# A hybrid attention layer on one core: the sample's dots in a pinned order, branch 3's loads, and three narrower products per sum of values

## The chip, the core and the metric

The kernel runs on one core of a Trainium2 chip. The metric is the device time of one launch in microseconds, the median of several runs. A core has five engines that work in their own order each: PE (TensorE, the matmuls), DVE (VectorE), ACT (ScalarE), POOL (GpSimd) and SP (SyncE, which here issues all transfers between the device's memory and the core's). An engine takes its instructions strictly in the order in which they stand; if the first of them waits, all behind it wait too.

## The reference, cut to what matters

One step of a one-layer decoder. 2048 prompt rows and 64 sample rows (8 sequences of 8) are normed and multiplied by one matrix; its columns feed an attention mixer of 8 heads (q, k, v), a gated linear attention (qb, kb, vb, g) and two gates; both mixers go through an output projection.

```python
DILATED = ((128, 1), (512, 4), (2048, 16))

def dilated_branch_sample(q, k_buf, v_buf, window, dil):
    ...
    idx = W + jnp.arange(T)[:, None] - dil * jnp.arange(n_keys)[None, :]
    ...
    kg = k_buf[:, idx]
    vg = v_buf[:, idx]
    s = jnp.einsum('bthd,btnhd->bthn', q, kg) * (hd ** -0.5)
    s = jnp.where(valid[None, :, None, :], s, -jnp.inf)
    return softmax_attend(s, vg, 'bthn,btnhd->bthd')

def dilated_mixture(results):
    outs = jnp.stack([r[0] for r in results], axis=0)
    lses = jnp.stack([r[1] for r in results], axis=0)
    alpha = jax.nn.softmax(lses, axis=0)
    return jnp.einsum('gblh,gblhd->blhd', alpha, outs)
```

The prompt is attended in the same three branches (window and dilation), each query with the keys of its own residue. For the sample, each of 64 rows is multiplied with the cached keys of its branch: those dots, for branches 2 and 3, are what the kernel calls `sample_scores`.

## The kernel before

The prompt is worked in 16 tiles of 128 rows and in four groups `m` of four tiles. `project` multiplies a tile with one column block: 8 steps of K, three matmuls each, since every number is held as a high and a low half in f16 (high x high, high x low, low x high). `first(m)` runs the blocks v, q and k of a group; `rest` runs qkb, then g and vb in turn, then gb. Between the steps of `project`, `pump` advances the attention by one step, at a rate set by `credit` and by the shares given to `weave`.

Attention is a list of items. An item is `attend`: `qk` (L402) multiplies queries and keys on PE, takes mask and minimum on DVE (L416) and the exponential on ACT (L419); `tr` (L423) turns the probabilities on PE (L426) and splits them into two f16 halves, in turn by ACT and DVE (L388, L389) or by ACT and POOL (L391 to L393); `pv` (L436) multiplies them with the values (L441). A unit of branch 1 or 2 has two items of two heads, a residue of branch 3 two items of four heads; the pipeline holds three items at a time and runs an item's `pre` (its loads) one item ahead. The values lie in memory as 64 high and 64 low columns a head, so L441 multiplies 128 columns with the high and with the low half of the probabilities and leaves 128 columns, which `added` (L452) folds: ACT copies the low half (L457), DVE adds it to the high one (L458).

Branch 3 (`branch3`, L931) loads in `pre` a transposed tile of queries, one of keys and one of values, and swaps the halves of the queries on DVE (`swapped`, L845 and L846). Its pool has two buffers a tile.

The sample's dots are 64 turns (sequence b, row t). A turn loads the row's queries `qb` to all partitions (L990), the branch 3 keys `k3` (L992) and, every second turn, the branch 2 keys `k2` (L995); POOL multiplies into one buffer `pr` (L980), and DVE sums it over the 64 columns of a head (L981), first for branch 3, then for branch 2. `dot_next` takes one or two turns after each projection of groups 2 and 3, the rest run with `qkb`.

The order on each engine is not the order of the text: a scheduler places every instruction when its own timing has its inputs and buffers ready.

Of the kernel before, what the change touches and what calls it, by code (L numbers as in the profile page):

```python
# [18 lines left out]
P = 128  # L19
# [33 lines left out]
def tile_hymba(ctx: ExitStack, tc: tile.TileContext, A: dict):  # L53
# [52 lines left out]
    ident8 = cp.tile([P, P], F32, name="ident8")  # L106
    DVE.tensor_scalar(ident8[:], ident[:], 0.125, None, ALU.mult)

    ident64 = cp.tile([P, 64], F32, name="ident64")
    for r0 in (0, 64):  # L110
        DVE.tensor_copy(ident64[r0 : r0 + 64], ident8[r0 : r0 + 64, r0 : r0 + 64])
# [202 lines left out]
    def by16(ap, r):  # L314
        return ap.rearrange("(i r) c -> r i c", r=16)[r]
# [3 lines left out]
    def chain(*gens):  # L319
        for g in gens:  # L320
            yield from g
# [27 lines left out]
    with ExitStack() as c1:  # L349
# [45 lines left out]
        def attend(tag, nh, nb, scores, mask, vf, nmf, denf, OT, pre=None, post=None, neg=-1.0):  # L395
# [40 lines left out]
            def pv():  # L436
                for i in range(nh):
                    o_ = OT(i)
                    for n in range(2 * nb):
                        b, c = divmod(n, 2)  # L440
                        PE.matmul(  # L441
                            o_, t["pt"][:, c, (i * nb + b) * P : (i * nb + b + 1) * P], vf(i, b),
                            start=(n == 0), stop=(n == 2 * nb - 1),
                        )
# [7 lines left out]
        def added(out, O):  # L452

            o4 = O.rearrange("p (h c d) -> p h c d", c=2, d=HD)
            split_[0] += 2
            l = ptp.tile([P, 4, HD], F32, name=f"ol_{split_[0]}", tag="ol", bufs=1)
            ACT.activation(l[:], o4[:, :, 1], AF.Copy)  # L457
            DVE.tensor_tensor(out, o4[:, :, 0], l[:], ALU.add)  # L458


        xs, early = {}, []
# [381 lines left out]
        def swapped(q):  # L843

            DVE.tensor_copy(q[0:64, 1], q[64:128, 0])  # L845
            DVE.tensor_copy(q[64:128, 1], q[0:64, 0])  # L846
# [11 lines left out]
        def unit(m, pp, br, x):  # L858
# [30 lines left out]

            def OT(i):  # L890
                if "O" not in T:
                    T["O"] = ps_O.tile([P, 512], F32, name=f"O_{br}_{m}_{pp}_{x}", tag="O")
                return T["O"][:, i * P : i * P + P]
# [34 lines left out]
            return out  # L928


        def branch3(r):  # L931
            T = {}

            def pre():
                q = T["q"] = b3.tile([P, 2, NH, P], F16, name=f"T3_q_{r}", tag="Tq")
                SP.dma_start_transpose(q[:, 0], by16(qp_d, r))
                k = T["k"] = b3.tile([P, NH, P], F16, name=f"T3_k_{r}", tag="Tk")
                SP.dma_start_transpose(k[:], by16(kp_d, r))
                swapped(q)
                yield  # L940
                T["v"] = b3.tile([P, 1024], F16, name=f"v3_{r}", tag="v3")
                SP.dma_start(T["v"][:], by16(vp_d[:], r))
                T["o"] = b3.tile([P, NH, 66], F32, name=f"o3_{r}", tag="o3")

            def OT(a, i):
                if ("O", a) not in T:
                    T["O", a] = ps_O.tile([P, 512], F32, name=f"O3_{r}_{a}", tag="O")
                return T["O", a][:, i * P : i * P + P]

            def post(a):  # L950
                added(
                    T["o"][:].rearrange("p (i a) d -> p i a d", a=2)[:, :, a, 0:64], T["O", a][:]
                )
                if a:
                    SP.dma_start(by16(o3_d[:], r), T["o"][:].rearrange("p h d -> p (h d)"))

            return [
                attend(
                    f"3_{r}_{a}", 4, 1,
                    lambda i, a=a: [  # L960
                        (T["q"][:, order_, 2 * i + a], T["k"][:, 2 * i + a])
                        for order_ in range(2)
                    ],
                    m3,
                    lambda i, b, a=a: T["v"][:, (2 * i + a) * P : (2 * i + a + 1) * P],
                    lambda i, a=a: T["o"][:, 2 * i + a, 65:66],
                    lambda i, a=a: T["o"][:, 2 * i + a, 64:65],
                    lambda i, a=a: OT(a, i),
                    pre=None if a else pre, post=lambda a=a: post(a), neg=scl["s"][:],
                )  # L970
                for a in range(2)
            ]
# [2 lines left out]
        q_s = q_d[S : S + NS, :]  # L975
        sk_state = {}

        def dot(out, kt, qt, tag):
            pr = sk.tile([P, 512], F32, name=f"pr_{tag}", tag="pr", bufs=1)
            POOL.tensor_tensor(pr[:], kt, qt, ALU.mult)  # L980
            DVE.tensor_reduce(  # L981
                out, pr[:].rearrange("p (u k d) -> p u k d", u=2, k=4), AX.X, ALU.add
            )

        def sample_scores(b, t):
            if t == 0:
                sk_state["sc"] = sk.tile([P, 2, 64], F32, name=f"sck_{b}", tag="sc")
            sc = sk_state["sc"]
            qt = sk.tile([P, 512], F32, name=f"qb_{b}_{t}", tag="qbc")
            SP.dma_start(qt[:], q_s[8 * b + t : 8 * b + t + 1, :].to_broadcast([P, 512]))  # L990
            k3 = sk.tile([P, 512], F32, name=f"k3_{b}_{t}", tag="k3")
            SP.dma_start(k3[:], ck[b].rearrange("(m r) c -> r m c", r=16)[t])  # L992
            if t < 4:
                k2 = sk.tile([P, 512], F32, name=f"k2_{b}_{t}", tag="k2", bufs=1)
                SP.dma_start(k2[:], ck[b, W - 512 : W, :].rearrange("(j r) c -> r j c", r=4)[t])  # L995
                sk_state["k2"] = k2
            out = sc[:].rearrange("p g (u t k) -> p g t u k", u=2, t=8)[:, :, t]
            dot(out[:, 1], k3[:], qt[:], f"3_{b}_{t}")
            dot(out[:, 0], sk_state["k2"][:], qt[:], f"2_{b}_{t}")
            if t == 7:  # L1000
                SP.dma_start(sc_d[b * P : (b + 1) * P, :], sc[:].rearrange("p g c -> p (g c)"))

        nwa = kp.tile([P, KT], F32, name="nwa")
        ACT.activation(nwa[:], nw[:], AF.Abs)
# [10 lines left out]
        def q_place(k):  # L1015

            pool, tag = ((sp, "s"), (ptp, "pt"), (sk, "k3"))[k // 3]
            return pool.tile([P, 512], F32, name=f"wr_q_{k}", tag=tag)[:]

        fetch_w("q", places=q_place)  # L1020
        with tc.manual_schedule(engines={mybir.EngineType.Activation}):
# [40 lines left out]

        from collections import deque

        work, side = deque(), deque()

        def pipeline():

# [25 lines left out]
        def pump():  # L1094
            return next(pipe) is not False
# [34 lines left out]
            return (2 if name == "g" else 1) * (NT * KT + 2)  # L1130


        credit = rate = 0.0

        def dot_next(t):
            for _ in range(1 + (t != "s" and t % 2)):
                if side:
                    side.popleft()()

        def first(m):  # L1140
            tiles = list(range(4 * m, 4 * m + 4))
# [17 lines left out]
            for t in tiles:  # L1159
                for name in "vqk":  # L1160
                    if (name, t) == ("q", 15):
                        at_once(load_w("qkb"))
                    yield from project(name, [t])
                    dot_next(t)
                if t < 12:
                    prep(t + 4)
                if t < 8:
                    fetch(t + 8)
# [4 lines left out]
        for m in range(4):  # L1173
            for _ in first(m):
                credit += 3 * rate
                while credit >= 1:
                    credit -= 1
                    pump()
            for pp in range(2):
                for br in (1, 2):  # L1180
                    for x in range(4):
                        work.extend(unit(m, pp, br, x))
            rate = 0.62
            if m == 1:
                for b in range(8):
                    for t in (0, 4, 1, 5, 2, 6, 3, 7):
                        side.append(lambda b=b, t=t: sample_scores(b, t))
        c_first.close()


# [19 lines left out]
        def dots():  # L1210
            while side:
                side.popleft()()
                yield

        att = [attention(), 5.2 * len(work)]
        host = [rest("qkb"), steps("qkb")]
        weave(host, att, [chain(load_w("g"), load_w("vb")), 4 * KT], [dots(), len(side) + 3])
        c_b3.close()
        c_dot.close()
        c_att.close()  # L1220
# [667 lines left out]
```

## Time and profile before

| | us |
|---|---|
| median of 3 runs | 1423.52 (1422.46 to 1428.86) |
| the profiled execution, as a run | 1426.68 |
| its span in the trace | 1424.9 |
| mean granted clock of TensorE | 0.966 |
| idle time of POOL just before L980 | 184.9 |
| idle time of DVE just before L981 | 44.0 |

The page lists busy time by engine, the chain that ended last, and groups of instructions. In a group's row the name left of `<-` is what it writes, then its shape; behind the bar stand its busy time, the mean of one in ns, and the engine's idle time just before it with what ended most of it. Buffer numbers are left out, so `k` stands for `k2` and `k3`.

### The profile page before, as it was taken

What the parts mean: (1) busy time and instruction counts of PE and PEld (TensorE: products, weight loads), DVE (VectorE), ACT (ScalarE), POOL (GpSimd) and SP (SyncE); (2) the same over time, 40 slices, a digit from 0 to 9 for tenths busy, and PEclk for the clock granted to TensorE, in tenths of its full rate; (3) what the DMA queues carried; (4) which work ended last, traced back from release to release, by engine and by line L of the source; (5) the groups of instructions that cost most, each with busy time, mean ns of one, the idle gap of its engine ahead of it and who ended that gap; (6) DMA issues with size and microseconds to landing.
All of it is one profiled execution on the core that took longest, in us unless ns stands there. A gap on an engine that the chain in (4) does not pass through costs nothing.

```text
span 1424.9 us, 26506 instructions
## 1 busy us (share of the span) xinstructions
PE 1285.0 (90%) x8942; PEld 743.6 (52%) x8942; DVE 1018.0 (71%) x2459; ACT 843.7 (59%) x2259; POOL 621.9 (44%) x564
## 2 busy tenths in 40 slices
PE   5989999889898898996889999889999989999997
PEld 2434555455455554664667666666555434444343
DVE  6797697789798967666775357898877797773222
ACT  6466787667377775875677665777876542221120
POOL 0144355566577455554421486556551264340000
PEclk9999999999999899997999999999999999999998
DMA  8469756678966797888976444242235759998661
GB/s 297 156 188 255 192 161 150 182 203 215 240 165 173 208 288 239 260 217 228 234 190 179 149 123 116 87 153 91 88 119 176 267 179 344 359 316 267 221 215 63
DMA packets 246874, 283.27 MB, mean 199 GB/s; under 512 B 117889, under 2 KB 148690, under 8 KB 246738
## 3 DMA queue, kind: packets, MB, share of 16 engines
q1 hardware_dynamic: 246738, 281.57, 67.1%
q8 instruction: 71, 1.16, 0.4%
q14 instruction: 65, 0.53, 0.1%
HBM read 183.19 MB, written 75.24 MB: 181 GB/s over the span
## 4 chain that ended last, share of the span: by engine, by line
PE 35%; DVE 25%; DMA 16%; ACT 11%; issue 7%; POOL 4%; SPq 2%; DVEq 0%; POOLq 0%; ACTq 0%
PE Y L1488 7%; PE acc_g L1120 3%; PE acc_vb L1120 3%; PE acc_k L1120 3%; DMA k<-in_cache_k_win 2%; POOL pr L980 2%; PE s L408 2%; PE OS L1737 2%; PE acc_qkb L1120 2%; ACT p L419 2%; DMA o_d<-o 2%; DMA oc<-o_d 2%; DVE p L416 2%; PE acc_v L1120 2%; DMA T_q<-qp_d 2%
## 5 line engine op out<-in xcount | busy, mean ns | idle before, releaser
L980 POOL TENSOR_TENSOR pr<-k,qb 128x512 f32<-128x512 f32 x128 | 171.8, 1342 | 184.9 <-DVE sck L981 113.9
L1120 PEld LDWEIGHTS <-hr 128*128 128x128 f16 x1824 | 177.7, 100 | 138.2 <-issue 17.6
L419 ACT ACTIVATE p<-p,o 128x256 f32<-128x256 f32 (+1 forms) x384 | 173.1, 453 | 86.0 <-DVE o L416 83.3
L1120 PEld LDWEIGHTS <-hl 128*128 128x128 f16 x1248 | 123.2, 100 | 146.6 <-issue 22.2
L1488 PE MATMUL Y<-w_o,mh 128*128 128x512 f16 x768 | 182.9, 385 | 8.3 <-ACT mh L1454 4.9
L416 DVE CUSTOM_DVE_ANT_0 p<-s,m3w,scl_s 128x256 f32<-128x256 f32 (+1 forms) x384 | 143.6, 419 | 39.0 <-DMA o_d<-o 20.3
L393 POOL TENSOR_TENSOR pt<-p,pt 128x512 f16<-128x512 f32 (+1 forms) x80 | 98.3, 1229 | 139.6 <-ACT pt L392 107.3
L441 PE MATMUL O<-v,pt 128*128 128x128 f16 x1200 | 116.1, 224 | 25.3 <-POOL pt L393 10.0
L426 PE MATMUL t<-ident,p 128*128 128x128 f32 x600 | 119.0, 289 | 14.5 <-ACT p L419 9.2
L1488 PEld LDWEIGHTS <-mh 128*128 128x128 f16 x768 | 72.5, 99 | 103.7 <-issue 25.2
L408 PE MATMUL s<-kk,qq 128*128 128x256 f16 (+1 forms) x512 | 105.7, 326 | 17.5 <-DVE o L416 12.4
L981 DVE TENSOR_REDUCE sck<-pr 128x8 f32<-128x512 f32 x128 | 87.0, 680 | 44.0 <-POOL pr L980 43.7
L441 PEld LDWEIGHTS <-pt 128*128 128x128 f16 x1200 | 86.6, 101 | 54.6 <-POOL pt L393 13.6
L1120 PE MATMUL acc_g<-w_g,hr 128*128 128x272 f16 (+1 forms) x768 | 103.3, 285 | 1.9 <-DVE so_g L677 1.0
L1120 PE MATMUL acc_v<-w_v,hl 128*128 128x512 f16 x384 | 99.5, 405 | 4.6 <-DMA hl<-ht 3.7
L426 PEld LDWEIGHTS t<-ident,p 128*128 128x128 f32 x600 | 73.5, 146 | 43.2 <-ACT p L419 26.4
L1120 PE MATMUL acc_q<-w_q,hl 128*128 128x512 f16 x384 | 92.0, 380 | 1.9 <-ACT zs_q L703 1.4
L1120 PE MATMUL acc_k<-w_k,hl 128*128 128x512 f16 x384 | 91.3, 382 | 2.5 <-ACT w_k L658 1.3
L1454 ACT ACTIVATE mh<-tm 128x1024 f16<-128x1024 f16 x32 | 31.7, 1019 | 104.1 <-PE tm L1453 97.7
L1120 PE MATMUL acc_gb<-w_gb,hr 128*128 128x512 f16 x384 | 90.0, 388 | 2.1 <-DVE so_gb L677 2.1
L1120 PE MATMUL acc_vb<-w_vb,hr 128*128 128x512 f16 x384 | 89.3, 379 | 1.6 <-DVE so_g L677 1.6
L212 ACT ACTIVATE E<-D_e 128x256 f32<-128x256 f32 (+1 forms) x168 | 67.7, 411 | 27.1 <-DVE ks L219 17.6
(533 smaller groups left out, 2628.1 us busy)
## 6 DMA issues: line engine op xcount, KB each, us to landing
k<-in_cache_k_win SPq DMA_DIRECT2D x104, 256.0 KB, 4.3
sv<-in_cache_v_win SPq DMA_DIRECT2D x104, 256.0 KB, 5.4
hr<-h_d SPq DMA_DIRECT2D x44, 512.0 KB, 4.1
qb<-q_d SPq DMA_DIRECT2D x64, 256.0 KB, 4.6
oc<-o_d SPq DMA_DIRECT2D x48, 264.0 KB, 5.8
o_d<-o SPq DMA_DIRECT2D x64, 132.0 KB, 3.9
x<-in_x_prompt SPq DMA_DIRECT2D x16, 512.0 KB, 5.8
h_d<-hl SPq DMA_DIRECT2D x16, 512.0 KB, 4.7
```

The lines of the kernel that those rows point to most:

```text
L212: ACT.activation(E[rows, i, :n], D[rows, half], AF.Exp, scale=1.0 / 16.0)
L393: POOL.tensor_tensor(l, f, h, ALU.subtract)
L408: PE.matmul(s_ps[:, i * w : (i + 1) * w], q, k, start=(n == 0), stop=(n == len(prods) - 1),)
L416: DVE.tensor_tensor_reduce(s[:, sl], s_ps[:, sl], mask, neg, BIG, ALU.add, ALU.min, nmf(i))
L419: ACT.activation(s[:, sl], s[:, sl], AF.Exp, bias=nmf(i), scale=-1.0, accum_out=denf(i))
L426: PE.transpose(p_ps[:, i * P : (i + 1) * P], t["s"][:, i * P : (i + 1) * P], ident[:])
L441: PE.matmul(o_, t["pt"][:, c, (i * nb + b) * P : (i * nb + b + 1) * P], vf(i, b), start=(n == 0), stop=(n == 2 * nb - 1),)
L980: POOL.tensor_tensor(pr[:], kt, qt, ALU.mult)
L981: DVE.tensor_reduce(out, pr[:].rearrange("p (u k d) -> p u k d", u=2, k=4), AX.X, ALU.add)
L1120: PE.matmul(z, a_[:, k, :], w[:, p_, k, cols], start=(k == 0 and i == 0), stop=(k == KT - 1 and i == 2),)
L1454: ACT.activation(mhl[:, a], pt[:], AF.Copy)
L1488: PE.matmul(Y[:], a_[:, k, :], w_[:, part, k, :512], start=(i == 0), stop=(i == len(prods) - 1),)
```

## The change

Four things are edited, and a constant is built without a helper tile. First, the values: per block of keys three products of 64 columns (high x high, high x low, low x high) go to one 64-column sum, so `added` is gone and ACT copies the sum into `o`. The product of the two low halves is no longer formed.

```diff
             def pv():
...
-                    for n in range(2 * nb):
-                        b, c = divmod(n, 2)
+                    prods = [(b, *cd) for b in range(nb) for cd in ((0, 0), (0, 1), (1, 0))]
+                    for n, (b, c, d) in enumerate(prods):
                         PE.matmul(
-                            o_, t["pt"][:, c, (i * nb + b) * P : (i * nb + b + 1) * P], vf(i, b),
-                            start=(n == 0), stop=(n == 2 * nb - 1),
+                            o_, t["pt"][:, c, (i * nb + b) * P : (i * nb + b + 1) * P],
+                            vf(i, b)[:, d * HD : (d + 1) * HD],
+                            start=(n == 0), stop=(n == len(prods) - 1),
                         )
...
-            ACT.activation(l[:], o4[:, :, 1], AF.Copy)
-            DVE.tensor_tensor(out, o4[:, :, 0], l[:], ALU.add)
...
-                added(T["o"][:, :, 0:64], T["O"][:])
+                ACT.activation(T["o"][:, :, 0:64], T["O"][:], AF.Copy)
```

Second, branch 3 asks for a residue's tiles one residue (two items) earlier, and its values come as two tiles from the pool of branch 2's.

```diff
+        def load3(r):
+
+            T = T3[r] = {}
+            for nm_, src, shape in (("q", qp_d, [P, 2, NH, P]), ("k", kp_d, [P, 1, NH, P])):
+                t = T[nm_] = b3.tile(shape, F16, name=f"T3_{nm_}_{r}", tag=f"T{nm_}")
+                SP.dma_start_transpose(t[:, 0], by16(src, r))
+            T["v"] = []
+            for i in range(2):
+                v = vp.tile([P, 512], F16, name=f"v3_{r}_{i}", tag="v2", bufs=11)
+                SP.dma_start(v[:], by16(vp_d[:, 512 * i : 512 * i + 512], r))
...
             def pre():
-                q = T["q"] = b3.tile([P, 2, NH, P], F16, name=f"T3_q_{r}", tag="Tq")
-                SP.dma_start_transpose(q[:, 0], by16(qp_d, r))
...
+                if r == 0:
+                    load3(0)
+                    yield
+                T.update(T3[r])
+                swapped(T["q"])
+                if r < 15:
+                    load3(r + 1)
                 yield
```

Third, the dots are one generator: a turn sums the turn before, asks for the next turn's loads, and multiplies in place. Loads and sums are pinned: each stands on its engine behind all that the text has put on that engine so far.

```diff
+            def load(b, t):
+                qt = sk.tile([P, 512], F32, name=f"qb_{b}_{t}", tag="qbc", bufs=3)
+                k3 = sk.tile([P, 512], F32, name=f"k3_{b}_{t}", tag="k3", bufs=3)
...
+                for to, of in asked:
+                    tc.keep_in_program_order(SP.dma_start(to[:], of))
...
+                    tc.keep_in_program_order(
+                        DVE.tensor_reduce(
...
+            for i, (b, t) in enumerate(turns):
...
+                if last:
+                    sums(*last)
+                if i + 1 < len(turns):
+                    now = load(*turns[i + 1])
+                POOL.tensor_tensor(k3[:], k3[:], qt[:], ALU.mult)
+                POOL.tensor_tensor(qt[:], k2[:], qt[:], ALU.mult)
+                last = b, t, sc, (qt, k3)
+                yield
```

Turns are taken step by step, 1.5 to 8 steps of a projection, instead of one or two behind it. Fourth, in `rest` each further block runs a tile behind the first.

```diff
+                for g in side:
+                    dots += 1.5 / KT
+                    if dots >= 1:
+                        dots -= 1
+                        next(g, None)
...
-            for t in ["s"] + order[names[0]]:
-                for name in names:
-                    yield from project(name, [t])
+            tiles = ["s"] + order[names[0]]
+            for i in range(len(tiles) + len(names) - 1):
+                for j, name in enumerate(names):
+                    if 0 <= i - j < len(tiles):
+                        yield from project(name, [tiles[i - j]])
```

What this makes of the engines' order, at the places that the prediction speaks of. POOL, in the middle of the dots (sequence 4; `pt` is the low half of an item's probabilities), before:

```order
L980 TENSOR_TENSOR pr_3_4_4_5873<-k3_4_4_5871,qb_4_4_5869 128x512
L393 TENSOR_TENSOR pt_1_3_0_0_1_6478<-p_1_3_0_0_1_6389,pt_1_3_0_0_1_6478 128x512
L980 TENSOR_TENSOR pr_2_4_4_5876<-k2_4_0_5861,qb_4_4_5869 128x512
L980 TENSOR_TENSOR pr_3_4_1_6014<-k3_4_1_6010,qb_4_1_6008 128x512
L393 TENSOR_TENSOR pt_1_3_0_1_1_6566<-p_1_3_0_1_1_6486,pt_1_3_0_1_1_6566 128x512
L980 TENSOR_TENSOR pr_2_4_1_6017<-k2_4_1_6012,qb_4_1_6008 128x512
```

and now:

```order
L1033 TENSOR_TENSOR k3_4_4_5975<-k3_4_4_5975,qb_4_4_5974 128x512
L1034 TENSOR_TENSOR qb_4_4_5974<-k2_4_0_5816,qb_4_4_5974 128x512
L1033 TENSOR_TENSOR k3_4_1_6059<-k3_4_1_6059,qb_4_1_6058 128x512
L1034 TENSOR_TENSOR qb_4_1_6058<-k2_4_1_6060,qb_4_1_6058 128x512
L393 TENSOR_TENSOR pt_2_2_1_0_1_6219<-p_2_2_1_0_1_6084,pt_2_2_1_0_1_6219 128x512
L1033 TENSOR_TENSOR k3_4_5_6167<-k3_4_5_6167,qb_4_5_6166 128x512
```

The products no longer share a buffer, and no row of POOL needs a sum of the row ahead of it. DVE at the same turns, before (L458 is the add, L981 a sum):

```order
L389 SCALAR_TENSOR_TENSOR pt_1_3_0_1_0_6518<-t_1_3_0_1_0_6510,pt_1_3_0_1_0_6518 128x512
L458 TENSOR_TENSOR o_1_3_0_0_6317<-O_1_3_0_0_6498,ol_197_6554 128x4x64
L981 TENSOR_REDUCE sck_4_5856<-pr_3_4_1_6014 128x2x4
L416 ISA p_1_3_0_3_0_6610,o_1_3_0_3_6585<-s_1_3_0_3_0_6609,m3w_404,scl_s_410 128x256
L416 ISA o_1_3_0_3_6585 128x1
```

and now:

```order
L1012 TENSOR_REDUCE sck_4_5970<-qb_4_4_5974 128x2x4
L1012 TENSOR_REDUCE sck_4_5970<-k3_4_4_5975 128x2x4
L416 ISA p_2_2_1_2_0_6293,o_2_2_1_2_6263<-s_2_2_1_2_0_6292,m3w_402,scl_s_408 128x256
L416 ISA o_2_2_1_2_6263 128x1
L416 ISA p_2_2_1_2_0_6293,o_2_2_1_2_6263<-s_2_2_1_2_0_6292,m3w_402,scl_s_408 128x256
L416 ISA o_2_2_1_2_6263 128x1
L389 SCALAR_TENSOR_TENSOR pt_2_2_1_1_0_6286<-t_2_2_1_1_0_6281,pt_2_2_1_1_0_6286 128x512
L1012 TENSOR_REDUCE sck_4_5970<-qb_4_1_6058 128x2x4
L1012 TENSOR_REDUCE sck_4_5970<-k3_4_1_6059 128x2x4
```

The two sums of a turn now stand together, and the add is gone. DVE in branch 3, where the queries are swapped, before (residue 10, behind the last score step of residue 8):

```order
L416 ISA o3_8_8776 128x1
L677 TENSOR_SCALAR so_g02_10388<-acc_g0_2_10358,wi_g_6800 128x256
L845 COPY T3_q_10_8981<-T3_q_10_8981 64x1024
L846 COPY T3_q_10_8981<-T3_q_10_8981 64x1024
L458 TENSOR_TENSOR o3_7_8661<-O3_7_0_8886,ol_302_8898 128x4x64
```

and now (residue 4, behind that of residue 2):

```order
L416 ISA p_3_2_1_8385,o3_2_8300<-s_3_2_1_8384,m3w_402,scl_s_408 128x128
L416 ISA o3_2_8300 128x1
L838 COPY T3_q_4_8407<-T3_q_4_8407 64x1024
L839 COPY T3_q_4_8407<-T3_q_4_8407 64x1024
L823 TENSOR_TENSOR za_0_9949<-za_0_9949,acc_g0_s_9932 64x272
L389 SCALAR_TENSOR_TENSOR pt_3_2_0_8454<-t_3_2_0_8443,pt_3_2_0_8454 128x512
```

The swap keeps its distance of two residues. SP, a stretch of the dots now (`qb`, `k3`, `k2` are the loads of turns 4, 1 and 5 of sequence 4):

```order
L891 DMA o1_d_67<-o_1_2_1_2_5718 128x264
L594 DMA wr_g_2_6245<-in_w_in 128x528 x2
L931 DMA_TRANSPOSE T3_k_1_8047<-kp_d_73 128x8x128
L1018 DMA sc_d_70<-sck_3_5166 128x128
L1005 DMA qb_4_4_5974<-q_d_58 128x512
L1005 DMA k3_4_4_5975<-in_cache_k_win 128x512
L1005 DMA qb_4_1_6058<-q_d_58 128x512
L1005 DMA k3_4_1_6059<-in_cache_k_win 128x512
L1005 DMA k2_4_1_6060<-in_cache_k_win 128x512
L594 DMA wr_g_4_6248<-in_w_in 128x528
L1005 DMA qb_4_5_6166<-q_d_58 128x512
L1005 DMA k3_4_5_6167<-in_cache_k_win 128x512
```

A turn's loads now stand together, behind the stores that the text put ahead of them.

More of the change, by code (lines that the diff above doesn't have):

```diff
@@ L450, in attend @@
             return [pre, qk, tr, pv]
[L452 to L458, printed above, removed]
         xs, early = {}, []
@@ L976, in tile_hymba @@
         sk_state = {}
[L978 to L1001, printed above, removed]
@@ L1063, in tile_hymba @@
         from collections import deque
-        work, side = deque(), deque()
+        work, side = deque(), []
         def pipeline():
@@ L1130, in steps, with counted @@
             return (2 if name == "g" else 1) * (NT * KT + 2)
[L1133 to L1138, printed above, removed]
+        credit = rate = dots = 0.0
+        taken = [0]
+        def counted(gen):
+            for _ in gen:
+                taken[0] += 1
+                yield
         def first(m):
@@ L1163, in first @@
                     yield from project(name, [t])
-                    dot_next(t)
                 if t < 12:
@@ L1184, in tile_hymba @@
             if m == 1:
-                for b in range(8):
-                    for t in (0, 4, 1, 5, 2, 6, 3, 7):
-                        side.append(lambda b=b, t=t: sample_scores(b, t))
+                side.append(counted(sample_scores()))
         c_first.close()
```

72 lines of the change are left out of this document (49 added, 23 removed).

## The prediction

> **What bounds the kernel now.** I read the page's engine line first, then the chain that ended last, and then asked for the stages in which the edited code runs.
>
> ```profile
> span 1424.9 us, 26506 instructions
> PE 1285.0 (90%) x8942; PEld 743.6 (52%) x8942; DVE 1018.0 (71%) x2459; ACT 843.7 (59%) x2259; POOL 621.9 (44%) x564
> PE 35%; DVE 25%; DMA 16%; ACT 11%; issue 7%; POOL 4%; SPq 2%; DVEq 0%; POOLq 0%; ACTq 0%
> PE Y L1488 7%; PE acc_g L1120 3%; PE acc_vb L1120 3%; PE acc_k L1120 3%; DMA k<-in_cache_k_win 2%; POOL pr L980 2%; PE s L408 2%; PE OS L1737 2%; PE acc_qkb L1120 2%; ACT p L419 2%; DMA o_d<-o 2%; DMA oc<-o_d 2%; DVE p L416 2%; PE acc_v L1120 2%; DMA T_q<-qp_d 2%
> ```
>
> PE is busy for nine tenths of the span, but it carries only 35% of the chain; DVE carries 25%, and the cache-key loads, the products `pr` and the branch 3 query loads `T_q` hold about 2% each. So PE is the busiest engine and is still held up by others. The stages tell where. Columns: stretch, length, then busy time of PE, PEld, DVE, ACT and POOL, the clock that TensorE was granted, the DMA share and GB/s.
>
> ```profile
> 100.00:200.00 100.00, 92.45 (x564) 51.56 (x565) 77.71 (x195) 69.84 (x199) 40.92 (x34) 0.97 0.81 214
> 200.00:460.00 260.00, 235.88 (x1545) 139.37 (x1543) 218.18 (x500) 178.28 (x505) 162.85 (x122) 0.97 0.72 188
> 460.00:640.00 180.00, 166.06 (x1153) 103.23 (x1152) 131.96 (x347) 127.97 (x365) 97.42 (x78) 0.95 0.84 240
> 640.00:760.00 120.00, 98.08 (x786) 69.48 (x784) 83.33 (x289) 81.48 (x283) 42.52 (x34) 0.90 0.84 211
> 760.00:810.00 50.00, 49.27 (x435) 36.94 (x434) 24.41 (x105) 37.82 (x131) 13.62 (x19) 1.00 0.52 150
> ```
>
> All five hold prompt attention; the sample's dots run only in the middle three. From 200 to 760 us PE is busy 235.9 + 166.1 + 98.1 = 500.0 of 560 us (89%), so 60 us are idle, and the clock was granted short by 0.03, 0.05 and 0.10 of those stretches, 7.8 + 9 + 12 = 29 us more. Together this is the pot that better order can win. Attention without dots loses less: 7.6% of PE's time at 100 to 200 us, where DVE is 78% busy, and 1.5% at 760 to 810 us, where DVE is 49% busy. What PE waits for from 200 to 760 us:
>
> ```profile
> PE s L408 <- DVE o L416: 12.7, 13, 2.3
> PE O L441 <- POOL pt L393: 8.4, 10, 2.4
> PE t L426 <- ACT p L419: 7.9, 6, 5.3
> PE O L441 <- DVE pt L389: 6.7, 5, 3.0
> ```
>
> (us in total, times, longest.) These are the score steps on DVE, the exponentials behind them, and the two ways of splitting the probabilities. None is edited; what is edited stands ahead of them on the same in-order engines. In the same stretch:
>
> ```profile
> DVE sck L981 <- POOL pr L980: 43.7, 43, 4.5
> DVE T_q L845 <- DMA T_q<-qp_d: 17.1, 8, 5.2
> DVE o L458 <- ACT ol L457: 9.6, 8, 2.3
> POOL pr L980 <- DVE sck L981: 113.9, 67, 5.9
> POOL pr L980 <- DMA k<-in_cache_k_win: 41.0, 14, 5.6
> POOL pr L980 <- DMA qb<-q_d: 6.8, 4, 3.0
> ```
>
> **Three 64-column products instead of two of 128.** 600 key blocks now take 1800 products where they took 1200, each with a weight load of its own. What counts is the pace from start to start.
>
> ```profile
> 577.20 0.61 PE L441 MATMUL O<-v,pt 128*128 128x128 f16 x8
> 561.72 0.22 PE L441 MATMUL O<-v,pt 128*128 128x128 f16 x1
> 922.49 1.15 PE L247 MATMUL sc_e<-qbd,ks 128*64 128x64 f32 x32
> ```
>
> Eight products take 0.61 us with the last one's 0.22: (0.61 - 0.22) / 7 = 0.056 us each, so 1200 x 0.056 = 67 us now. No 64-column f16 product is in the trace. Below, the cost is half the columns, 0.028 us (50 us); above, the weight load sets the pace and it stays 0.056 us (101 us). The nearest row that brings a new weight load with every 64-column product is the third, in f32 and two products side by side: (1.15 - 0.22) / 31 = 0.030 us for a load and a product. I take 0.030: 54 us, 13 saved, of which PE's 89% lets 12 through. The Trainium skill ("TensorE: Matmul & The Clock Gate", "Back-to-back issue gap") speaks against it: a stream of loads and products is to hold about 81 ns each at 128 columns. The trace disagrees with 56 ns; if a load's surplus of 25 ns did come on top of the 30, the term would be 1800 x 0.055 = 99 us, a rival below.
>
> **The add on DVE goes.** Where ACT copied half of O (L457) and DVE added the other half (L458), ACT now copies the whole result.
>
> ```profile
> L458 DVE TENSOR_TENSOR o<-O,ol 128x256 f32<-128x256 f32 x96 | 40.0, 417 | 20.8 <-ACT ol L457 20.6
> L457 ACT ACTIVATE ol<-O 128x256 f32<-128x256 f32 x96 | 35.7, 372 | 22.5 <-PE O L441 12.5 <-DVE o L458 8.8 <-PE s L408 0.9
> ```
>
> ACT makes as many copies of the same shape, so nothing there. DVE loses 40.0 us of work, 5.6% of the 710 us of the five stages, and its waits of 20.6 us. None of this is on PE; it reaches PE through shorter waits for the rows L416 and L389.
>
> **The dots.** Work stays: 128 products and 128 sums.
>
> ```profile
> L980 POOL TENSOR_TENSOR pr<-k,qb x128: 1259/1272/2260, 239.0 to 724.9; 128x512 f32<-128x512 f32 x128
> k<-in_cache_k_win SPq DMA_DIRECT2D x104, 256.0 KB, 4.3
> qb<-q_d SPq DMA_DIRECT2D x64, 256.0 KB, 4.6
> ```
>
> 64 turns in 486 us make a turn of 7.6 us. One `pr` buffer ties POOL and DVE to each other twice a turn: 113.9 us and 43.7 us above. With products in place both ties go, and a sum stands a turn after its product: 2 x 1.27 us of POOL against 7.6 us. A load asked for a turn ahead has 7.6 us for 4.3 to 4.6. The new wait: loads are pinned on SP behind the store of `o` traced ahead of them, and behind them stand the reloads `hr` and stores; three buffers let a load wait only for sums of two turns back. I take these waits at nothing, and their bounds from nothing to what they are today. POOL's freedom brings `pt` (L393) earlier, 8.4 us of PE's waits.
>
> **Branch 3 two items ahead.** The sequence does not bear this out for the queries. `T_q` keeps two buffers, so the load for residue 4 waits for residue 2's scores, and on DVE its swap stands right behind residue 2's last score step, as before.
>
> ```profile
> DMA to landing us min/median/max: 3.4/4.1/7.7
> L416 DVE CUSTOM_DVE_ANT_0 p<-s,m3w,scl_s 128x128 f32<-128x128 f32 x168 | 48.7, 345 | 13.0 <-DMA o_d<-o 11.2 <-PE O L441 1.3 <-POOL pt L393 0.3
> ```
>
> Four score steps at 0.345 us cover 1.4 us of a landing of 4.1. So I keep the 17.1 us of DVE's waits; at best they go. The values come earlier, but no row shows a wait for them.
>
> **At nothing.** The constant that is built without `ident8`: one DVE operation, ahead of everything. 16 more loads, since branch 3's values come in halves. The spread of turns over the projections: as many turns per stage. The gate projection `g` running one tile ahead of `vb`: same products; a reload `hr` now waits for one more projection on SP, and the row
>
> ```profile
> SPq L565 <- PE acc_vb L1120: 8.9, 7, 2.3
> ```
>
> shows SP waiting like that already, while the reload runs three tiles ahead and no row of PE waits for `hr`.
>
> **The sum.** DVE's share from 200 to 760 us is 433.5 / 560 = 77.4%; without the add some 71.8%. On the line through the two dot-free stages (78%: 7.6%, 49%: 1.5%) that means 6.3% of idle PE, 35 us of 560, so 25 of the 60 come back if the dots no longer hold anyone. Queries still do: 17.1 us of DVE at PE's idle per DVE's idle, 60 / 126.5 = 0.47, is 8 us. That leaves 17. The clock would move from 0.97, 0.95, 0.90 toward 0.975, 15 us; since slow stretches lie around idle time already counted, I take a third, 5. So 12 + 17 + 5 = 34 us off the profiled execution's 1426.7, 1392.7; that run lies 3.2 us above the median of 1423.5, so **1389.5** on the scale of the median, say 1389.
>
> **Rivals.**
> Everything goes (14%): queries wait no more and idle PE falls to the 1.5% of 760 to 810 us: 52 + 12 + 10 us, 1350. For it: POOL and DVE lose all their mutual waits. Against: ACT's rows stay as they are.
> The pinned order waits (13%): sums or loads come late because products stand on POOL behind `pt`, which waits for ACT. If a turn's sums wait 1.3 us, DVE loses 83 us instead of 43.7, 39 x 0.47 = 18 us against 12 + 7 for products and add: 1422, no change. Under 0.7 us a turn it is today's cost.
> Weight loads set the pace (11%), the slower side: at 0.056 us the products add 34 x 0.89 = 30 us against 17 + 5: 1431. It decides from (67 + 25) / 1800 = 0.051 us on. Against: the f32 row at 0.030; for: no f16 row.
> Otherwise the forecast (62%), by itself 1370 to 1404: its lower end with 20 us more of the idle pot, its upper end with the dots' share halved and no clock.
>
> The range leaves out the slower rival and half of the best one, 18%: 1355 to 1424. A change under 0.5%, 7 us, this measurement can hardly tell from none. Faster by more: 62 + 14, plus 1 of the second rival, 77%; within: 12%; slower: 11%.
>
> **What would show it.** In the new profile: the 64-column products at about 0.030 us (x8 in some 0.43 us); no row of `pr` waiting for `sck`, and `sck` waiting for POOL well under 43.7 us; `T_q` still near 17 us; PE's idle time in the dots' stages down by a third; TensorE's clock above 0.95 there. Wrong if the product pace is over 0.05 us, if SP's pinned loads leave POOL waiting for DMA as long as the 47.8 us of today, or if the reload of `hr` shows up in front of `acc_g`.

## The result and the profile after

| | before | after |
|---|---|---|
| median, us | 1423.67 (1422.46 to 1428.86, 4 runs) | 1443.69 (1441.61 to 1446.92, 4 runs) |
| profiled execution, span, us | 1424.9 | 1445.1 |
| mean granted clock | 0.966 | 0.955 |

After to before is 1.0134, with a 95% interval of 1.0117 to 1.0152: 1.3% slower, where 1389 us were predicted. The page's first lines and its chain, after:

```profile
span 1445.1 us, 27602 instructions
PE 1281.6 (89%) x9542; PEld 740.1 (51%) x9542; DVE 993.1 (69%) x2362; ACT 844.1 (58%) x2259; POOL 623.5 (43%) x564
PE 34%; DVE 19%; DMA 12%; ACT 9%; issue 6%; POOL 4%; SPq 2%; DVEq 0%; POOLq 0%; ACTq 0%
PE Y L1526 11%; DMA k<-in_cache_k_win 5%; PE acc_vb L1157 3%; PE acc_qkb L1157 3%; PE OS L1775 3%; PE s L408 2%; DVE p L416 2%; ACT p L419 2%; PE acc_g L1157 2%; DMA o_d<-o 2%; DVE sck L1012 2%; DVE qbd L223 2%; PE t L426 1%; DMA ga_d<-so_g 1%; ACT E L212 1%
```

PE and DVE do less than before (1281.6 and 993.1 us of work against 1285.0 and 1018.0), and the span is 20 us longer. What grew is waiting, and the chain says for what: the cached keys hold 5% of it, where they held 2%.

The next two fences cut each trace at the last product of attention (the last `O` of L441). Columns: stretch, length, busy time of PE, PEld, DVE, ACT and POOL, clock, DMA share, GB/s. First the kernel before, then the changed one.

```profile
200.00:803.50 603.50, 542.79 (x3859) 344.07 (x3857) 456.98 (x1237) 422.64 (x1270) 312.73 (x247) 0.95 0.76 206
803.50:1424.90 621.40, 572.27 (x4138) 311.37 (x4136) 406.52 (x852) 294.88 (x687) 248.77 (x257) 0.97 0.58 188
```

```profile
200.00:817.30 617.30, 527.76 (x4291) 331.12 (x4289) 429.41 (x1127) 413.47 (x1241) 310.76 (x237) 0.93 0.74 200
817.30:1445.10 627.80, 581.04 (x4174) 316.11 (x4172) 412.74 (x854) 298.65 (x693) 254.45 (x264) 0.97 0.58 187
```

From 200 us to the end of attention PE is busy 15.0 us less (542.8 - 527.8), and the rows of L441 alone, the narrower products, take 86.2 us there where they took 104.6. PE is idle 28.8 us more (617.3 - 527.8 = 89.5 against 603.5 - 542.8 = 60.7). Together that makes 13.8 of the 20 us; another 6.4 us come behind. The waits from 200 to 760 us in the changed kernel (us in total, times, longest), of PE, DVE and POOL:

```profile
PE O L441 <- POOL pt L393: 29.8, 17, 5.2
PE s L408 <- DVE o L416: 19.4, 14, 3.2
DVE sck L1012 <- POOL qb L1034: 39.9, 22, 4.3
DVE p L416 <- POOL pt L393: 24.7, 9, 7.2
DVE T_q L838 <- DMA T_q<-qp_d: 13.7, 6, 4.9
POOL k L1033 <- DMA k<-in_cache_k_win: 127.9, 38, 15.1
POOL k L1033 <- DVE sck L1012: 6.2, 1, 6.2
```

POOL no longer waits for the sums (6.2 us, where it was 113.9), as the edit intends. It waits for keys instead: 127.9 us against 41.0. And the row that grows most on PE is the split of the probabilities on POOL, `pt` L393: 29.8 us against 8.4. One place shows how these belong together. Two splits get their last input when ACT's L392 ends, at 311.28 and 313.74 us (timelines of ACT, POOL, DVE and PE; start, duration, and in brackets the idle time before and its releaser):

```profile
310.65 0.63 ACT L392 ACTIVATE pt<-p 128x512 f16<-128x512 f32 x1
313.12 0.62 ACT L392 ACTIVATE pt<-p 128x512 f16<-128x512 f32 x1
320.23 0.51 ACT L419 ACTIVATE p<-p,o 128x256 f32<-128x256 f32 x1 [6.49 <-DVE o L416]
```

```profile
317.30 1.26 POOL L1033 TENSOR_TENSOR k<-k,qb 128x512 f32<-128x512 f32 x1 [15.05 <-DMA k<-in_cache_k_win]
318.52 1.15 POOL L393 TENSOR_TENSOR pt<-p,pt 128x512 f16<-128x512 f32 x1
319.63 1.28 POOL L1034 TENSOR_TENSOR qb<-k,qb 128x512 f32<-128x512 f32 x1
320.86 2.50 POOL L1033 TENSOR_TENSOR k<-k,qb 128x512 f32<-128x512 f32 x2
323.32 1.16 POOL L393 TENSOR_TENSOR pt<-p,pt 128x512 f16<-128x512 f32 x1
```

```profile
319.71 0.48 DVE L416 CUSTOM_DVE_ANT_0 p<-s,m3w,scl_s 128x256 f32<-128x256 f32 x1 [7.22 <-POOL pt L393]
```

```profile
319.73 1.25 PE L441 MATMUL O<-v,pt 128*128 128x64 f16 x20 [4.07 <-POOL pt L393]
```

POOL stands for 15 us at a product whose keys have not come. The first split is behind it and starts 7.2 us after its input; the second stands behind three further products and starts 9.6 us late. Behind the first split PE waits 4.1 us and DVE 7.2 us, whose next score step writes into a buffer `p` that the split still reads; ACT waits 6.5 us for that step. So the sample's dots, which are background work here, hold up attention on three engines.

For all runs below I counted this: from the end of ACT's L392 to the start of the split L393 that it feeds, paired in order, for all splits between 200 and 760 us. Before, 65 splits start 52.9 us late in all, 29.0 us of it while a product of the dots runs; after, 62 splits start 170.5 us late, 91.9 us of it while a product runs. I call this the **lateness of the splits**.

### The profile page after: what moved, and what is told of

Its sections match the earlier page's. It is cut to its first block, busy times and chain, and to the rows that moved or that the text cites. A ratio compares the mean times of both kernels' runs of the same rounds, so it can differ in the third digit from the quotient of the medians.

```text
span 1445.1 us, 27602 instructions
## 1 busy us (share of the span) xinstructions
PE 1281.6 (89%) x9542; PEld 740.1 (51%) x9542; DVE 993.1 (69%) x2362; ACT 844.1 (58%) x2259; POOL 623.5 (43%) x564
## 4 chain that ended last, share of the span: by engine, by line
PE 34%; DVE 19%; DMA 12%; ACT 9%; issue 6%; POOL 4%; SPq 2%; DVEq 0%; POOLq 0%; ACTq 0%
PE Y L1526 11%; DMA k<-in_cache_k_win 5%; PE acc_vb L1157 3%; PE acc_qkb L1157 3%; PE OS L1775 3%; PE s L408 2%; DVE p L416 2%; ACT p L419 2%; PE acc_g L1157 2%; DMA o_d<-o 2%; DVE sck L1012 2%; DVE qbd L223 2%; PE t L426 1%; DMA ga_d<-so_g 1%; ACT E L212 1%
## 5 line engine op out<-in xcount | busy, mean ns | idle before, releaser
L393 POOL TENSOR_TENSOR pt<-p,pt 128x512 f16<-128x512 f32 (+1 forms) x80 | 95.2, 1191 | 186.0 <-ACT pt L392 155.2
L1033 POOL TENSOR_TENSOR k<-k,qb 128x512 f32<-128x512 f32 x64 | 86.7, 1357 | 146.5 <-DMA k<-in_cache_k_win 127.9
L441 PE MATMUL O<-v,pt 128*128 128x64 f16 x1800 | 98.7, 198 | 44.5 <-POOL pt L393 30.5
L441 PEld LDWEIGHTS <-pt 128*128 128x128 f16 x1800 | 86.5, 102 | 80.9 <-POOL pt L393 35.6
L408 PE MATMUL s<-kk,qq 128*128 128x256 f16 (+1 forms) x512 | 107.4, 332 | 21.2 <-DVE o L416 15.0
L1034 POOL TENSOR_TENSOR qb<-k,qb 128x512 f32<-128x512 f32 x64 | 87.9, 1378 | 4.1 <-DMA k<-in_cache_k_win 1.7
```

What stands on the lines that cost most here:

```text
L393: POOL.tensor_tensor(l, f, h, ALU.subtract)
L408: PE.matmul(s_ps[:, i * w : (i + 1) * w], q, k, start=(n == 0), stop=(n == len(prods) - 1),)
L441: PE.matmul(o_, t["pt"][:, c, (i * nb + b) * P : (i * nb + b + 1) * P], vf(i, b)[:, d * HD : (d + 1) * HD], start=(n == 0), stop=(n == len ...
L1033: POOL.tensor_tensor(k3[:], k3[:], qt[:], ALU.mult)
L1034: POOL.tensor_tensor(qt[:], k2[:], qt[:], ALU.mult)
```

## The experiments

The theories: **1** the pin of the loads on SP makes keys late; **2** the pin of the sums holds DVE; **3** the turns stand too dense or in the wrong places; **4** without the buffer `pr` nothing holds the products back, and they pile up ahead of the splits on POOL. Ratios are to runs of the kernel before on the same chip, with their 95% interval. All times are medians.

**Parts undone, and one part alone.** In `free_loads`:

```diff
-                    tc.keep_in_program_order(SP.dma_start(to[:], of))
+                    SP.dma_start(to[:], of)
```

> The changed kernel with one thing undone: the turns' loads of queries and cache keys are no longer pinned on SP; the sums stay pinned on DVE. Theory 1 (the pin makes the loads late: on SP they stand behind stores that wait for ACT, DVE and PE, POOL's products wait 127.9 us for keys where it was 41.0, the splits `pt` of attention stand behind them on POOL, and TensorE waits 30.5 us for those instead of 10.0): POOL's wait for keys falls below 60 us, TensorE's for `pt` of POOL below 15 us, and the time to 1425 us or less. Theory 2 (the pinned sums on DVE hold the score steps): the time stays within 7 us of 1444. Theory 3 (the turns stand too dense beside the projections whatever queue they use): within 7 us of 1444 too, with POOL's waits lower all the same.

1440.4 us, ratio 1.0113 (1.0083 to 1.0142). From 200 to 760 us POOL still waits 124.6 us for keys and PE 22.1 us for POOL's splits, and the lateness is 141 us. The pin is not what makes POOL wait; theory 1 falls as the main cause.

In `old_dots` the code of the dots, of `dot_next` and of their place in `weave` is that of the kernel before.

> The changed kernel with the whole of the dots as before: one buffer `pr` for the products, loads in the turn that uses them, nothing pinned, a turn or two after each projection; the three 64-column products, branch 3 two items ahead and the stagger stay. If the dots alone make the change slower (theories 1 to 3), the rest is a gain: 1400 to 1415 us. If the stagger of `vb` behind `g` or branch 3's loads cost something too, it stays above 1424.

1402.3 us, ratio 0.9846 (0.9815 to 0.9876); lateness 62 us. So the dots' part costs 41 us, and the rest of the change is a gain of 1.5%.

In `pv_alone` the kernel before gets the three products and ACT's copy (first diff of the change) and nothing else.

> The kernel before with one part of the change alone: three products of 64 columns for a key block, and ACT's copy of the whole of O in place of the copy and the add on DVE. In the changed kernel's trace the products start every 28 to 29 ns, 1800 x 0.0285 = 51 us instead of 67: if what PE saves and DVE's 40 us come through as the prediction had it, 1424 - 16 x 0.89 - 7 = about 1403, at least 1395 to 1415. If TensorE's time saved here is lost again in waits for the steps of the softmax: within 7 us of 1424.

1407.1 us, ratio 0.9887 (0.9859 to 0.9915): 16 us gained by the ratio, within the range that was expected.

In `no_stagger`:

```diff
-            tiles = ["s"] + order[names[0]]
-            for i in range(len(tiles) + len(names) - 1):
-                for j, name in enumerate(names):
-                    if 0 <= i - j < len(tiles):
-                        yield from project(name, [tiles[i - j]])
+            for t in ["s"] + order[names[0]]:
+                for name in names:
+                    yield from project(name, [t])
```

> The changed kernel with `g` and `vb` of one tile projected one after the other, as before. In the changed kernel's trace the last product of `vb` comes 36 us later than before, while the last of `g` comes 23 us later. If the stagger costs time of its own: 1444 - 8 to -15 = 1429 to 1436. If it only moves `vb` back, and the lag was there already at 460 us (10 to 16 us): within 5 us of 1444.

1432.9 us (1428.0 to 1443.7, 7 runs), ratio 1.0051 (1.0016 to 1.0086). The median is 11 us better, with runs spread over 16 us. The lateness is 171 us, as in the changed kernel. The stagger is taken up again below.

**What of the dots.** In `tied` the loads stay a turn ahead and pinned, but each product goes into one buffer again, with its sum behind it and unpinned. Queries and keys have two buffers each here, three in the changed kernel:

```diff
-                POOL.tensor_tensor(k3[:], k3[:], qt[:], ALU.mult)
-                POOL.tensor_tensor(qt[:], k2[:], qt[:], ALU.mult)
-                last = b, t, sc, (qt, k3)
+                dot(out[:, 1], k3[:], qt[:], f"3_{b}_{t}")
+                dot(out[:, 0], k2[:], qt[:], f"2_{b}_{t}")
...
+                pr = sk.tile([P, 512], F32, name=f"pr_{tag}", tag="pr", bufs=1)
+                POOL.tensor_tensor(pr[:], kt, qt, ALU.mult)
```

> The changed kernel with one buffer `pr` for the products again: each product waits for the sum of the one before it, the sums stand in the turn itself and are not pinned; loads of keys and queries stay a turn ahead and pinned on SP, with two buffers each. Theory 4 (without that buffer nothing holds the products back, they stand ahead of the splits `pt` on POOL: in the changed kernel the 62 splits of 200 to 760 us start 170 us in all after their input from ACT, 92 us of it behind products, in the one before 53 us and 29 us): POOL's order is loosened again, the splits' lateness falls below 90 us, and the time comes to 1400 to 1415 us as with the whole of the dots as before (1402). Theory 1 again (pinned loads): stays above 1425. Theory 2 (the pinned sums): also 1400 to 1420, so the run with nothing pinned has to tell the two apart.

1403.3 us, ratio 0.9833 (0.9809 to 0.9858); lateness 73 us. All 41 us are back. The waits of PE and POOL from 200 to 760 us in this version:

```profile
PE O L441 <- POOL pt L393: 1.8, 3, 0.8
POOL pr L1010 <- DVE sck L1011: 133.0, 70, 4.7
POOL pr L1010 <- DMA k<-in_cache_k_win: 37.8, 15, 3.8
```

POOL waits 133.0 us for sums, more than in the kernel before, and PE hardly waits for POOL any more.

In `no_pins` both pins are gone, products stay in place:

> The changed kernel with neither loads nor sums pinned; products in place, loads a turn ahead in the text, sums a turn behind. Theory 2 (the pinned sums hold DVE, as the loads were shown to do little by themselves): 1400 to 1415 us. Theory 4 (products pile up ahead of the splits on POOL): 1430 us or more, since the products are as free as before.

1438.9 us, ratio 1.0068 (1.0037 to 1.0099); lateness 129 us. Theory 2 falls as the main cause. Here the last sum ends at 616 us, where it ended at 723 us in the changed kernel: left alone, the dots run ahead of attention. PE's own rows look different from those of the changed kernel (200 to 760 us):

```profile
PE s L408 <- DVE o L416: 24.2, 20, 2.6
PE O L441 <- POOL pt L393: 10.9, 7, 2.7
```

The wait for POOL's splits is near that of the kernel before (8.4 us), and the wait for the score steps on DVE is longer. Part of the loss is busy time as well: from 200 us to the end of attention PE is busy 539.5 us at a granted clock of 0.92, where `tied` is busy 523.2 us at 0.95 with about as many matmuls. So one row of PE doesn't tell the whole cost.

In `pin_products`:

```diff
-                POOL.tensor_tensor(k3[:], k3[:], qt[:], ALU.mult)
-                POOL.tensor_tensor(qt[:], k2[:], qt[:], ALU.mult)
+                tc.keep_in_program_order(POOL.tensor_tensor(k3[:], k3[:], qt[:], ALU.mult))
+                tc.keep_in_program_order(POOL.tensor_tensor(qt[:], k2[:], qt[:], ALU.mult))
```

> The changed kernel with the products pinned on POOL as well, each behind all that stands ahead of it in the program, the splits of attention among them. Theory 4: the splits no longer stand behind products that were written after them, their lateness falls from 170 us to 60 to 110 us and the time to 1405 to 1425. Theory 2 or a cost of the loads: stays within 7 us of 1444, since sums and loads stand as they did.

1414.4 us, ratio 0.9919 (0.9892 to 0.9945); lateness 99 us. A second way of keeping the products behind the splits, with nothing else changed, wins 29 us. The waits from 200 to 760 us:

```profile
PE O L441 <- POOL pt L393: 10.8, 10, 2.1
DVE sck L1012 <- POOL qb L1034: 37.4, 16, 6.4
POOL k L1033 <- DMA k<-in_cache_k_win: 80.0, 23, 12.6
```

PE's wait for the splits falls from 29.8 to 10.8 us, while DVE waits for the products about as long as before the pin (37.4 against 39.9).

In `old_turns` the generator is advanced once or twice behind each projection, as `dot_next` was, in place of 1.5 times in 8 steps:

> The changed kernel with the turns of the first projections where they were: one after each projection, two after those of the tiles with odd numbers, in place of an even spread over the steps. If the spread puts pinned loads and sums between steps of attention where they stop SP and DVE: 5 to 20 us faster, 1424 to 1439. If the place of a turn doesn't matter: within 5 us of 1444.

1430.4 us (1421.3 to 1432.1, 10 runs), ratio 1.0011 (0.9988 to 1.0034); lateness 122 us. The spread costs 13 us, so theory 3 holds in part, but the version remains 27 us above `tied`, which keeps the spread.

**Work or waiting, and small parts.** In `short_products` both products cover 64 of 512 columns, so the sample's scores are left mostly unmultiplied; POOL's busy time from 200 to 760 us falls from 303.5 to 175.3 us, 1.0 us a product.

> The changed kernel with products over 64 of the 512 columns (the sums run over all of them, so the sample's scores come from keys and queries mostly unmultiplied: that part of the computation is left out); loads, pins, order in the text and sums stay. It takes some 60 products' worth of work, 128 x about 1.1 us, off POOL and leaves the waits for keys. If the splits are late because of the work of the products ahead of them (92 us of 170): TensorE's wait for POOL's splits falls below 12 us and the time to 1400 to 1420. If they are late because POOL stands waiting for keys ahead of them: within 10 us of 1444.

1418.5 us, ratio 0.9950 (0.9927 to 0.9972): the time came as for the work, PE's wait for POOL's splits did not (23.2 us). The lateness falls to 79 us, of which 16 us lie beside products. What is left, 43 us as in the changed kernel, is POOL standing idle ahead of a split. Both kinds, work and waiting for keys, delay it.

`tied_no_stagger`, `tied_own_b3` and `tied_free` each change `tied` in one thing: the stagger undone as above; `load3(r)` called in the residue that uses it; the loads unpinned as above.

> The version with one product buffer (1403 us) and besides `g` and `vb` of one tile projected one after the other, as before. In the changed kernel the stagger seemed to cost 11 us, with a wide spread of its runs. If it costs by itself: 1390 to 1397. If it is worth nothing either way, as the prediction had it: within 5 us of 1403.

> The version with one product buffer (1403 us) and besides branch 3's loads asked for in the item that uses them, as before (its values still in halves). If the loads two items ahead bring nothing, as the prediction had it (their queries wait for a buffer all the same): within 5 us of 1403, DVE's wait for `T_q` between 10 and 20 us as in the changed kernel (13.7). If they do bring time: 1408 to 1420 and a longer wait for `T_q`.

> The version with one product buffer (1403 us) and besides the turns' loads not pinned on SP. If the pins cost nothing where the buffer holds the products back: within 5 us of 1403. If they cost the 4 us that they seemed to cost in the changed kernel, or more: 1395 to 1399.

1400.8 us (ratio 0.9832, 0.9794 to 0.9869), 1406.4 (0.9875, 0.9840 to 0.9910) and 1394.7 (0.9789, 0.9751 to 0.9827). Without the early loads DVE waits 19.5 us for `T_q`, with them 19.9 in `tied`: the loads of branch 3 bring 3 us by the medians and 6 by the ratios, inside the intervals. The pin of the loads costs about 9 us by the medians and 6 by the ratios once the products are tied, and the intervals just overlap; the lateness goes from 73 to 50 us.

**What the buffer is worth by itself.** `sums_in_turn` undoes the delay and the pin of the sums and leaves products in place; `sums_in_turn_2` has two buffers each for queries and keys besides, so that against `tied` it differs in nothing but this and in the text's order, where both sums stand behind both products:

```diff
-                pr = sk.tile([P, 512], F32, name=f"pr_{tag}", tag="pr", bufs=1)
-                POOL.tensor_tensor(pr[:], kt, qt, ALU.mult)
...
+                POOL.tensor_tensor(k3[:], k3[:], qt[:], ALU.mult)
+                POOL.tensor_tensor(qt[:], k2[:], qt[:], ALU.mult)
```

> The changed kernel with the sums in the turn of their products and not pinned; products in place, loads a turn ahead and pinned. If the missing buffer alone lets the products pile up (theory 4): 1430 to 1445, the splits' lateness over 110 us. If it is the delay of the sums that costs: 1402 to 1415.

> The version with one product buffer (1403 us) and one thing changed: each product is written over its own input instead of into `pr`, so that no product waits for the sum of another; two buffers each for queries and keys, sums in the turn and not pinned, loads a turn ahead and pinned, all as there. If the one buffer is what keeps the products from standing ahead of the splits: 1425 to 1445, the splits' lateness over 100 us. If the number of query and key buffers (three in the changed kernel, two here) was what mattered: 1400 to 1412.

1440.4 us (ratio 1.0089, 1.0060 to 1.0117) and 1437.8 (1.0080, 1.0055 to 1.0105), lateness 105 and 108 us, the first a little under the 110 that were expected. The waits of PE from 200 to 760 us in `sums_in_turn_2`:

```profile
PE O L441 <- POOL pt L393: 21.2, 15, 4.5
PE s L408 <- DVE o L416: 12.8, 10, 2.9
```

21.2 us for POOL's splits, against 1.8 in `tied`. The buffer alone is worth 34 us. This pair doesn't show that all of it goes through the splits: DVE's sums also wait longer for products here (80.8 us for `k` and 12.2 for `qb`, 55.3 in `tied`), and a product in place keeps its input's buffer from the next load until it is summed. A third buffer for queries and keys (`sums_in_turn`, 1440 us) brought nothing. In `pin_products`, where products are in place too, DVE's wait hardly changed, and 29 us came back.

Theory 4 is about order, and the order can be counted. Of the 128 products, those that stand three or more in a row on POOL with no split between them are 99 in the changed kernel and 69 in the one before. In all versions whose products are in place and not pinned they are 81 to 105 (102 in `sums_in_turn_2`); with one product buffer or pinned products they are 60 to 69 (68 in `tied`, 65 in `pin_products`). PE's idle time from 200 us to the end of attention falls into the same two groups: 78 to 93 us for free products of full length, 69 for the short ones, and 49 to 69 where products are held back. So what the fast versions share is that products are held back among the splits.

`pinned_prod_free_loads` is `pin_products` with the loads unpinned.

> The changed kernel with the products pinned on POOL (1414 us) and the loads not pinned on SP. If the loads' pin costs what it cost in the version with one buffer (1403 to 1395, 9 us): 1402 to 1408, about the time with the dots as before. If the 12 us that pinned products leave against 1402 are the sums a turn behind: within 4 us of 1414.

1413.4 us, ratio 0.9897 (0.9859 to 0.9935). Its lateness is 50 us, the same as that of `tied_free`, and it is 19 us slower than that. So the lateness is not the whole account, and it does not rank the versions either: it is 99 us in `pin_products` at 1414 us and 105 in `sums_in_turn` at 1440. Of the 41 us that the dots cost, the 11 by which pinned products stay above `old_dots` are unexplained. They are not the pin of the loads. The sums a turn behind are left as a candidate, which no run isolates where the products are held back.

**The best version.** `tied_free` with the stagger undone:

> The fastest version so far (one product buffer, loads not pinned, 1395 us) and besides `g` and `vb` of one tile one after the other. If the stagger is worth nothing: within 5 us of 1395; if it costs a little, as two runs hinted (11 and 3 us): 1384 to 1392.

1388.1 us (1384.9 to 1398.4, 5 runs), ratio 0.9729 (0.9703 to 0.9756), 2.7% faster than the kernel before, and the fastest seen. Undoing the stagger won 11, 3 and 7 us by the medians in three pairs of versions, 12, 0 and 9 by the ratios; the single runs of each pair overlap, so that it costs a few us is likely, not settled.

## Why the prediction was wrong

By its own steps, in order:

- **Products: right.** In the changed kernel's timeline of PE twelve of them take 0.51 us:

```profile
562.16 0.51 PE L441 MATMUL O<-v,pt 128*128 128x64 f16 x12
L441 PE MATMUL O<-v,pt x1800: 189/193/262, 122.7 to 817.1; 128*128 128x64 f16 x180
```

With the last one's 0.193, (0.51 - 0.193) / 11 = 0.029 us each, where 0.030 was taken. PE's busy time fell by 15.0 us up to the end of attention (13 forecast), and with the add gone from DVE the part by itself gained 16 us (`pv_alone`). The rival in which weight loads set the pace is out. The rule of the Trainium skill weighed there ("TensorE: Matmul & The Clock Gate", "Back-to-back issue gap") gives 81 ns for a load and a product of 128 columns; its other formula in that section, columns / 2.4 + 2.5 ns, meant for a product by itself with no time for a load, would give 29 ns at 64 columns as an estimate, and that is what the trace has with a load each.
- **The dots: this is the step that failed.** It said that with products in place both ties go, that the new waits cost nothing, and that "POOL's freedom brings `pt` (L393) earlier". The tie of POOL to DVE's sums did go; DVE's wait for the products stayed (39.9 us against 43.7). But the tie was also what held the products back in POOL's order: with one buffer a product could be placed only behind the sum of the one before it, and splits were placed in between. Free, the products stand in longer rows ahead of the splits, working or waiting for keys, and the splits come 170 us late where it was 53. Of PE's idle time 17 us were to be won; it grew by 29 up to the end of attention, and the dots' part cost 41 us. The run that gives the buffer back and the run that pins the products show it; the pair `tied` and `sums_in_turn_2` puts 34 us on the buffer alone. How much of it goes through the splits in each version stays open.
- **The waits taken at nothing.** The bound was "what they are today", 47.8 us of POOL waiting for transfers. It became 127.9 for keys alone, past the upper bound and past the mark that the prediction set for itself. That number is not the loss, though: with nothing pinned POOL waits 16.9 us for keys and 38.3 for queries, and the time is still 1439. In the place shown above, what costs is the split that stands behind the wait.
- **The rival of the pinned order** (13%) had the right engine and the wrong order and price. It put products behind `pt`; it is `pt` that stands behind products. It priced the waits of the sums on DVE, which stayed, and so came to no change.
- **Branch 3: right.** `T_q` waits 13.7 us (17.1 forecast), and undoing the early loads changes the time by less than the intervals show.
- **At nothing:** the stagger costs 3 to 11 us by the medians (0 to 12 by the ratios), the spread of turns 13 us while the products are free, where nothing was put. PE shows no wait for `hr`; its rows for `acc_g` wait for ACT, 4.6 us.
- **Clock: wrong sign.** 5 us were to come back with less idle time. Idle time grew, and the granted clock from 200 us to the end of attention fell from 0.95 to 0.93.

Taken together, by the ratios: -16 us from the products and the add, another -6 from all else but the dots (`old_dots` stands at -22), and +41 from the dots make the +19 of 1.0134. The 6 are within the intervals of the two runs.

## What to carry to other kernels

A long wait on an engine with time to spare can be what keeps its queue in a useful order: before you remove it, ask what the freed instructions will stand ahead of, and who waits for that. If background work shares an in-order engine with work on the critical path, hold it back on that engine, by one buffer or by a pin (here the version with the buffer was 11 us faster than the one with the pin), and price a change of its order at the engine behind it, not by its own waits. Where a change has several parts, time them apart: here one part's 16 us were hidden by another's 41.

## What was not expected of the hardware

The same 104 loads of 256 KB of cached keys land later when they are pinned. In the changed kernel the median from issue to landing is 5.8 us; with the loads unpinned it is 4.9. With one product buffer it is 5.3 us pinned and 4.5 unpinned, with pinned products 5.6 and 4.9; in the kernel before it is 4.3. With neither loads nor sums pinned (`no_pins`) it is 5.2, so the pin is not all that counts. The rows are those of the changed kernel, of `free_loads`, `tied` and `tied_free`:

```profile
k<-in_cache_k_win SPq DMA_DIRECT2D x104, 256.0 KB, 5.8
```

```profile
k<-in_cache_k_win SPq DMA_DIRECT2D x104, 256.0 KB, 4.9
```

```profile
k<-in_cache_k_win SPq DMA_DIRECT2D x104, 256.0 KB, 5.3
```

```profile
k<-in_cache_k_win SPq DMA_DIRECT2D x104, 256.0 KB, 4.5
```

Pinned loads are issued in groups, the first eight of keys and queries between 238.4 and 241.6 us, so they may share the transfer engines with each other; no run isolates that.
